# Expert tiles from a transposed copy in memory, and gate one-hots made eight tokens at a time with the gates multiplied in on ScalarE

## The chip, the cores and the metric

The kernel runs on one core of a Trainium2 chip. The metric is the device time of one execution in microseconds. A number comes from three executions and from one profiled execution.

## What is computed

One layer of an encoder for 1024 tokens of width 1024 in float32: attention heads, a recurrent group, and then a retrieval layer (PEER), which the change is about. For each token, 8 heads pick 16 each of 16384 experts; an expert is one row of `expert_u` and one row of `expert_v`.

```python
e_idx = i1[top] * 128 + i2[top]            # 8 heads x 16 experts of each token
gate = softmax(top_s)
u = take(expert_u, ic)                     # (tokens, 128, 1024)
act = gelu(einsum('cd,ced->ce', xc, u))
vv = take(expert_v, ic)
y = einsum('ce,ced->cd', gc * act, vv)
```

## The kernel before

The work up to the retrieval layer is not touched (lines up to 1323). The retrieval layer handles its tokens in two ways. Three blocks of 128 tokens (`NGB = 3`) are gathered: `gather_tasks` (1355) fetches for token block and expert slot the 128 rows of `peer_u` that its tokens chose by an indirect DMA from GpSimd (`fetch`, 1359), multiplies and sums them on VectorE (1392), and adds 128 rows of `peer_v`, scaled, to an accumulator (1400). That makes 384 steps with a u fetch and a v fetch each; `gathers` hands them out in portions.

The other five blocks (640 tokens, `TD`) go the dense way: every one of the 16384 experts is evaluated for every token, and the gates, zero for an expert that was not chosen, decide what counts. The experts come as 128 tiles of 128. A tile is handled so:

- `u_load` (1437) brings 128 rows of `peer_u` (128x1024) on SP's queue; two buffers.
- `u_transpose` (1442) turns half of it, four 128x128 pieces, on TensorE into a PSUM bank named `put` (tag `a`, one of three banks that `pact` uses too); ScalarE copies the bank to `uTh` as rounded float32r (1452), VectorE subtracts that from the bank and leaves the remainder in `uTl` (1458).
- `act_half` (1460) makes for half of the 640 tokens the products uTh x dTh, uTh x dTl and uTl x dTh over 8 pieces (lines 317 to 319, tile `pact`), and ScalarE puts Gelu of them into `gl` (1467). For the 65 tiles named `early` the result goes to memory (`actd`).

`tile_steps` (1471) lists the steps of one tile with the load of the tile after next and the transposes of the next tile in it.

`merge` lays several lists of steps over each other, each over a given share of the whole; the order of the steps, and with it the order of each engine's instructions, comes from these lists, which a scheduling layer then follows closely. Four stretches follow each other, with times as in the profile:

1. About 1180 to 1360: queries of the first three blocks.
2. About 1360 to 1950: queries of the others, the lists of chosen experts (`c_steps`), 45 early tiles and the first 74 gather steps.
3. About 1950 to 2380, the gate stage: `g_steps` (1690) makes the dense table of gates in memory, `Gd`, block by block; 20 early tiles and 60 gather steps run beside it.
4. From 2380, the dense stage: the remaining 63 tiles, `gate` (1790: GpSimd multiplies `gl` with the table, ScalarE and VectorE split it into `ah` and `al`), and the products with the v tiles (`one`, 1823, tile `py`, lines 1835 to 1837), which VectorE adds up every four tiles (1844). GpSimd makes the remainder `vl` of each v tile (1815). The gathers go on.

In `g_steps` an expert number is taken apart into row i and column j of a 128x128 grid, and for one token the gates are the product of two one-hot matrices with the 128 chosen experts as the contracted index: `o1` holds the gate where the row matches, `o2` a 1 where the column matches. `prep` makes the transposed tables `tT` (rows, columns, gates, and the negated gates and rows). `hot` (1710) makes the one-hots of eight tokens; `mm` (1733) makes eight 128x128 products (1741) into two PSUM banks `pgb`, from which ScalarE copies them into `st` (1744); `store` writes `st` to `Gd`. There are 80 such groups of eight, and two buffers of `o1` and `o2` each.

The work of `hot` is shared out: all eight `o2` at once on VectorE (1714); of the eight `o1` four on VectorE, two on GpSimd (1720), two on ScalarE, as an absolute value and then a Relu (1726, 1730). `MIX` says which:

```python
MIX = "DDDDPPAA"
eng = nc.vector if MIX[q] == "D" else nc.gpsimd
r_ = eng.tensor_scalar(o1[:, q], io128, tT[:, 0, t:t + 1], tT[:, 2, t:t + 1],
                       op0=ALU.is_equal, op1=ALU.mult)
if MIX[q] == "P":
    pace[0] = r_
```

`pace[0]` is the last GpSimd operation recorded; `fetch` orders each gather behind it on GpSimd, without a wait, so that gathers are spread over the stage. During the gate stage a gather has seven buffers for u and seven for v (four, and three more for this stage), later four each.

## Time and profile before

| | |
|---|---|
| three executions | 4042.25, 4057.2, 4059.28 us |
| median | 4057.2 us |
| profiled execution: its own time | 4056.53 us |
| profiled execution: its span | 4054.8 us |
| busy share of the span | TensorE 86%, VectorE 75%, GpSimd 57%, ScalarE 31% |
| mean granted clock of TensorE | 0.928 of full speed |
| moved between memory and the core | 862.81 MB, mean 213 GB/s |

PE is TensorE, DVE VectorE, ACT ScalarE, POOL GpSimd, and SP the queue of most loads and stores. A group of instructions is named by line, engine, operation and tiles, as out<-in, and given with its count, busy time, the mean of one and the idle time of its engine just before. Matrix products overlap in the engine's pipe, so their busy time is less than count times mean. The shares are means over stretches that differ; the stretches are read apart.

### The profile page before, as it was taken

The numbers are of one execution on the slowest core, as the hardware profiler recorded it, in microseconds if no ns is written. First come the engines' busy times: TensorE is split into PE (matmuls) and PEld (weight loads), VectorE is DVE, ScalarE is ACT, GpSimd is POOL, SyncE is SP. The second block draws the span as 40 slices with busy tenths as digits, with TensorE's granted clock in tenths as the row PEclk, the third lists the DMA queues.
The fourth block names the chain that finished last, engine by engine and source line by source line (L and its number), as shares of the span: only waits on it lengthen the run. The fifth ranks groups of instructions, "written<-read, shape, count | busy, mean of one in ns | idle before, by whom it ended". The sixth has DMA issues, their size and how long they took to land. (4 is left out here: it accounts for less than half of the span.)

```text
span 4054.8 us, 62013 instructions
## 1 busy us (share of the span) xinstructions
PE 3468.1 (86%) x22961; PEld 3038.1 (75%) x22961; DVE 3047.6 (75%) x6082; ACT 1261.6 (31%) x2528; POOL 2316.8 (57%) x1762
## 2 busy tenths in 40 slices
PE   5978899988787878988888878889888988889898
PEld 4757877776787877878877766777777877777787
DVE  6776556776567999799788877777677878877765
ACT  3244344444213222222555532221222222222221
POOL 2132112221434466366699978777777877878774
PEclk9978998888898989999999989999899999999999
DMA  6543444343445366466798998777788888777774
GB/s 191 178 144 103 141 116 98 97 111 104 136 164 184 104 219 238 141 218 214 239 296 278 301 309 277 264 259 269 255 273 285 281 272 275 272 265 271 256 258 154
DMA packets 493462, 862.81 MB, mean 213 GB/s; under 512 B 149348, under 2 KB 290404, under 8 KB 489064
## 3 DMA queue, kind: packets, MB, share of 16 engines
q1 hardware_dynamic: 372840, 447.20, 34.3%
q0 software_dynamic: 113280, 411.63, 29.7%
q8 instruction: 181, 2.97, 0.3%
q10 hardware_dynamic: 7040, 0.03, 0.1%
q14 instruction: 121, 0.99, 0.1%
HBM read 741.91 MB, written 116.80 MB: 212 GB/s over the span
## 5 line engine op out<-in xcount | busy, mean ns | idle before, releaser
L1392 DVE SCALAR_TENSOR_TENSOR gu<-gu,ghr 128x1024 f32<-128x1024 f32 x384 | 590.3, 1538 | 301.5 <-DMA gu<-in_peer_u_dram,ei 296.2
L317 PE MATMUL pact<-dTh,uTh 128*128 128x320 f32 x2048 | 663.6, 324 | 72.2 <-DVE uTl L1458 68.3
L1400 DVE SCALAR_TENSOR_TENSOR gacc<-gv,gact,gacc 128x1024 f32<-128x1024 f32 x381 | 614.0, 1611 | 117.1 <-DMA gv<-in_peer_v_dram,ei 116.1
L319 PE MATMUL pact<-dTh,uTl 128*128 128x320 f32 x2048 | 651.3, 318 | 19.2 <-DVE uTl L1458 19.2
L318 PE MATMUL pact<-dTl,uTh 128*128 128x320 f32 x2048 | 650.3, 318 | 0.0
L1835 PE MATMUL py<-vh,ah 128*128 128x512 f32 x1280 | 531.7, 419 | 137.5 <-DVE yac L1844 77.4
L1364 POOL DMA_INDIRECT gu<-in_peer_u_dram,ei x384 | 517.9, 1349 | 86.2 <-issue 44.2
L1836 PE MATMUL py<-vl,ah 128*128 128x512 f32 x1280 | 529.1, 413 | 38.2 <-POOL vl L1815 38.2
L1364 POOL DMA_INDIRECT gv<-in_peer_v_dram,ei x384 | 477.9, 1245 | 115.0 <-issue 101.5
L1837 PE MATMUL py<-vh,al 128*128 128x512 f32 x1280 | 523.7, 409 | 4.5 <-DVE al L1796 4.5
L317 PEld LDWEIGHTS pact<-dTh,uTh 128*128 128x128 f32 x2048 | 400.8, 196 | 89.4 <-DVE uTl L1458 78.5
L1815 POOL TENSOR_TENSOR vl<-vr,vh 128x512 fp32r<-128x512 f32 x256 | 367.2, 1435 | 146.1 <-issue 116.5
L1835 PEld LDWEIGHTS py<-vh,ah 128*128 128x128 f32 x1280 | 254.9, 199 | 218.0 <-ACT vh L1814 68.8
L319 PEld LDWEIGHTS pact<-dTh,uTl 128*128 128x128 f32 x2048 | 400.1, 195 | 21.4 <-DVE uTl L1458 21.3
L318 PEld LDWEIGHTS pact<-dTl,uTh 128*128 128x128 f32 x2048 | 400.6, 196 | 2.6
L1836 PEld LDWEIGHTS py<-vl,ah 128*128 128x128 f32 x1280 | 255.2, 199 | 99.6 <-POOL vl L1815 51.4
L1467 ACT ACTIVATE gl<-pact 128x320 f32<-128x320 f32 x256 | 111.2, 437 | 632.8 <-PE pact L319 601.1
L1837 PEld LDWEIGHTS py<-vh,al 128*128 128x128 f32 x1280 | 255.2, 199 | 62.0 <-DVE al L1796 6.8
L1795 ACT ACTIVATE ah<-gl 128x640 fp32r<-128x640 f32 x128 | 92.7, 737 | 653.6 <-POOL gl L1794 552.0
L1720 POOL TENSOR_SCALAR o<-io,tT 128x128 f32<-128x128 f32 x160 | 232.5, 1457 | 35.7 <-ACT tT L164 27.5
L1741 PE MATMUL pgb<-o,o 128*128 128x128 f32 x1280 | 184.0, 290 | 64.8 <-POOL o L1720 56.4
L1814 ACT ACTIVATE vh<-vr 128x512 fp32r<-128x512 f32 x256 | 157.0, 624 | 226.3 <-PE py L1837 181.8
(1445 smaller groups left out, 7527.1 us busy)
## 6 DMA issues: line engine op xcount, KB each, us to landing
u<-in_peer_u_dram SPq DMA_DIRECT2D x128, 512.0 KB, 5.8
vr<-in_peer_v_dram SPq DMA_DIRECT2D x256, 256.0 KB, 4.0
Gd<-st SPq DMA_DIRECT2D x160, 256.0 KB, 7.1
actd<-gl SPq DMA_DIRECT2D x65, 320.0 KB, 4.4
gl<-actd SPq DMA_DIRECT2D x65, 320.0 KB, 4.8
awt<-in_ada_w_dram SPq DMA_DIRECT2D x32, 512.0 KB, 6.4
wraw<-in_peer_w_query_dram SPq DMA_DIRECT2D x32, 512.0 KB, 4.0
wraw<-in_w_in_dram SPq DMA_DIRECT2D x26, 512.0 KB, 5.1
```

What stands on the lines that cost most here:

```text
L317: nc.tensor.matmul(ps, lh, rh, start=(i == 0), stop=False)
L318: nc.tensor.matmul(ps, lh, rl, start=False, stop=False)
L319: nc.tensor.matmul(ps, ll, rh, start=False, stop=(i == n - 1))
L1364: g_ = nc.gpsimd.indirect_dma_start(out=r_, out_offset=None, in_=src, in_offset=bass.IndirectOffsetOnAxis(ap=eid[tb][:, j:j + 1], axis=0))
L1392: nc.vector.scalar_tensor_tensor(u, u, 1.0, hr, op0=ALU.mult, op1=ALU.mult, accum_out=act[:, q:q + 1])
L1400: nc.vector.scalar_tensor_tensor(acc, v, pact[:, q:q + 1], acc, op0=ALU.mult, op1=ALU.add)
L1720: r_ = eng.tensor_scalar(o1[:, q], io128, tT[:, 0, t:t + 1], tT[:, 2, t:t + 1], op0=ALU.is_equal, op1=ALU.mult)
L1741: nc.tensor.matmul(pg[:, q * 128:(q + 1) * 128], o1[:, 4 * x_ + q], o2[:, 4 * x_ + q], start=True, stop=True)
L1815: pace[0] = nc.gpsimd.tensor_tensor(vl, vts[i], vh, ALU.subtract)
L1835: nc.tensor.matmul(ys[hf][b], ah[:, ts], vh, start=(n == tiles[0]), stop=False)
L1836: nc.tensor.matmul(ys[hf][b], ah[:, ts], vl, start=False, stop=False)
L1837: nc.tensor.matmul(ys[hf][b], al[:, ts], vh, start=False, stop=(n == tiles[-1]))
```

## The change

The host makes a copy of `peer_u` in which tile n stands already transposed, as a new input (`in_peer_ut_dram`); `u_load` reads it, with 4 KB in each of 128 partitions as before. `u_split` takes the place of `u_transpose`: one copy of 128x1024 on ScalarE and one subtraction of 128x1024 on VectorE, from the loaded tile, and nothing on TensorE or in PSUM. In `hot` both one-hots are made by one wide comparison each on VectorE, and ScalarE multiplies the gate into each of the eight `o1` in place. GpSimd has no part in it, and `pace` is not set there. The gathers still read `peer_u` itself.

```diff
-ULP = (-1, 1)
-NUR = 1
-MIX = "DDDDPPAA"
...
         U, V = I["peer_u"][0], I["peer_v"][0]
-        Ue = U.rearrange("(a b) d -> b a d", b=128)
+        Ut = I["peer_ut"]
         Ve = V.rearrange("(a b) d -> b a d", b=128)
         TW = "tile"
         pe = ES()
...
                 next(gt, None)
-        uts, ats, urp = {}, {}, []
+        uts, ats = {}, {}
         early = [n for n in range(NT) if (n + 1) * NEARLY // NT > n * NEARLY // NT]
         seq = early + [n for n in range(NT) if n not in early]
         after = dict(zip(seq, seq[1:]))
         actd = dram.tile([NEARLY, 128, TD], F32, name="actd")
         def u_load(n):
+            if n in uts:
+                return
             u = lpa.tile([128, D], F32, name="u", bufs=NU)
-            nc.sync.dma_start(u, Ue[n])
+            nc.sync.dma_start(u, Ut[n])
             uts[n] = [u]
-        def u_transpose(n, kh):
-            if kh == 0:
-                uts[n] += [lpa.tile([128, NK, 128], FR, name="uTh"), lpa.tile([128, NK, 128], FR, name="uTl")]
-            u, uh, ul = uts[n]
-            pt = pa[0].tile([128, 512], F32, name="put", tag="a")
-            for i in range(4):
-                k = kh * 4 + i
-                nc.tensor.transpose(pt[:, i * 128:(i + 1) * 128], u[:, k * 128:(k + 1) * 128], ident)
-            ks = slice(kh * 4, kh * 4 + 4)
-            p3 = pt.rearrange("p (k e) -> p k e", k=4)
-            nc.scalar.activation(uh[:, ks], p3, AF.Copy)
-            if n in early and early.index(n) <= ULP[0] and kh >= ULP[1]:
-                ur = urp[0].tile([128, 512], F32, name="ur", bufs=NUR)
-                acp(ur, pt)
-                nc.gpsimd.tensor_tensor(ul[:, ks], ur.rearrange("p (k e) -> p k e", k=4), uh[:, ks], ALU.subtract)
-            else:
-                nc.vector.tensor_tensor(ul[:, ks], p3, uh[:, ks], ALU.subtract)
+        def u_split(n):
+            u_load(n)
+            if len(uts[n]) > 1:
+                return
+            u = uts[n][0]
+            uh, ul = lpa.tile([128, NK, 128], FR, name="uTh"), lpa.tile([128, NK, 128], FR, name="uTl")
+            u3 = u.rearrange("p (k e) -> p k e", k=NK)
+            nc.scalar.activation(uh, u3, AF.Copy)
+            nc.vector.tensor_tensor(ul, u3, uh, ALU.subtract)
+            uts[n] += [uh, ul]
         def act_half(n, hf):
+            u_split(n)
             _, uh, ul = uts[n]
             if hf == 0:
                 ats[n] = lpa.tile([128, TD], F32, name="gl", bufs=NGL)
...
             L = [lambda: act_half(n, 0), lambda: act_half(n, 1)]
             if n in after:
                 m = after[n]
-                L = [lambda: u_transpose(m, 0), L[0], lambda: u_transpose(m, 1), L[1]]
+                L = [lambda: u_split(m), L[0], lambda: None, L[1]]
                 if m in after:
-                    L[0] = lambda: (u_load(after[m]), u_transpose(m, 0))
+                    L[0] = lambda: (u_load(after[m]), u_split(m))
             return L
         with ES() as qs:
             q1 = qs.enter_context(tc.tile_pool(name="q1", bufs=1, reuse_waits=TW))
             q2 = qs.enter_context(tc.tile_pool(name="q2", bufs=2, reuse_waits=TW))
-            urp.append(q2)
             pq = qs.enter_context(tc.tile_pool(name="pq", bufs=5, space=PSUM, reuse_waits=TW))
             def qbank(name):
...
             for L in hl[:NGB]:
                 for f in L:
                     f()
-            u_transpose(seq[0], 0)
-            u_transpose(seq[0], 1)
+            u_split(seq[0])
             merge((Q1, 0, 1), (sum(hl[NGB:], []), 0.1, HE))
             cg, cd = [c_steps(tb) for tb in range(NGB)], [c_steps(tb) for tb in range(NGB, NB)]
             tl_ = [tile_steps(n) for n in early]
...
                     nc.tensor.transpose(pt[:, 128:256], fj[:, 1], ident)
                     nc.tensor.transpose(pt[:, 256:384], wgt[tb], ident)
-                    s["t"] = tT = g1.tile([128, 5, 128], F32, name="tT")
-                    acp(tT[:, 0:3].rearrange("p a b -> p (a b)"), pt[:, 0:384])
-                    nc.scalar.activation(tT[:, 3], pt[:, 256:384], AF.Copy, scale=-1.0)
-                    nc.scalar.activation(tT[:, 4], pt[:, 0:128], AF.Copy, scale=-1.0)
+                    s["t"] = tT = g1.tile([128, 3, 128], F32, name="tT")
+                    acp(tT.rearrange("p a b -> p (a b)"), pt[:, 0:384])
                 def hot(t8):
                     tT = s["t"]
                     t0 = t8 * 8
                     s[t8] = o1, o2 = [g1.tile([128, 8, 128], F32, name=n_, bufs=NHOT) for n_ in ("o1", "o2")]
-                    nc.vector.tensor_tensor(o2, io128[:, None, :].to_broadcast([128, 8, 128]),
-                                            tT[:, 1, t0:t0 + 8, None].to_broadcast([128, 8, 128]), ALU.is_equal)
+
+                    for i, o_ in enumerate((o1, o2)):
+                        nc.vector.tensor_tensor(o_, io128[:, None, :].to_broadcast([128, 8, 128]),
+                                                tT[:, i, t0:t0 + 8, None].to_broadcast([128, 8, 128]), ALU.is_equal)
                     for q in range(8):
-                        t = t0 + q
-                        if MIX[q] != "A":
-                            eng = nc.vector if MIX[q] == "D" else nc.gpsimd
-                            r_ = eng.tensor_scalar(o1[:, q], io128, tT[:, 0, t:t + 1], tT[:, 2, t:t + 1],
-                                                   op0=ALU.is_equal, op1=ALU.mult)
-                            if MIX[q] == "P":
-                                pace[0] = r_
-                        else:
-
-                            nc.scalar.activation(o1[:, q], io128, AF.Abs, bias=tT[:, 4, t:t + 1])
-                    for q in range(8):
-                        t = t0 + q
-                        if MIX[q] == "A":
-                            nc.scalar.activation(o1[:, q], o1[:, q], AF.Relu, scale=tT[:, 3, t:t + 1],
-                                                 bias=tT[:, 2, t:t + 1])
+                        nc.scalar.activation(o1[:, q], o1[:, q], AF.Copy, scale=tT[:, 2, t0 + q:t0 + q + 1])
                 def mm(t8):
                     if t8 % (TC // 8) == 0:
...
         a = _np.ascontiguousarray(inputs[name])
         arrays[f"in_{name}_dram"] = a
         args[name] = nc.dram_tensor(f"in_{name}_dram", a.shape, mybir.dt.from_np(a.dtype), kind="ExternalInput").ap()
+
+    a = inputs["peer_u"]
+    a = _np.ascontiguousarray(_np.asarray(a)[0].reshape(128, 128, NK, 128).transpose(1, 3, 2, 0)).reshape(128, 128, D)
+    arrays["in_peer_ut_dram"] = a
+    args["peer_ut"] = nc.dram_tensor("in_peer_ut_dram", a.shape, mybir.dt.from_np(a.dtype), kind="ExternalInput").ap()
     o = nc.dram_tensor("out_0_dram", (1, T, D), F32, kind="ExternalOutput").ap()
     with tile.TileContext(nc) as tc:
         body(tc, nc, args, o)
```

Two places of the order, in the gate stage. On POOL, GpSimd's queue, `o` is a tile of one-hots, and `gu` and `gv` are gathered rows. Before:

```order
L1364 DMA gv_21560<-in_peer_v_dram,ei0_11946 128x1024
L1720 TENSOR_SCALAR o1_21618<-io128_11962,tT_21614 128x128 x2
L1364 DMA gu_21642<-in_peer_u_dram,ei0_11946 128x1024
L1364 DMA gv_21644<-in_peer_v_dram,ei0_11946 128x1024
L1720 TENSOR_SCALAR o1_21648<-io128_11962,tT_21614 128x128 x2
L1720 TENSOR_SCALAR o1_21703<-io128_11962,tT_21614 128x128 x2
L1364 DMA gu_21718<-in_peer_u_dram,ei0_11946 128x1024
```

Now:

```order
L1361 DMA gv_19920<-in_peer_v_dram,ei0_11946 128x1024
L1361 DMA gu_19973<-in_peer_u_dram,ei0_11946 128x1024
L1361 DMA gv_19975<-in_peer_v_dram,ei0_11946 128x1024
L1361 DMA gu_20033<-in_peer_u_dram,ei0_11946 128x1024
L1361 DMA gv_20035<-in_peer_v_dram,ei0_11946 128x1024
L1361 DMA gu_20106<-in_peer_u_dram,ei0_11946 128x1024
```

The one-hots are gone from between the gathers; 65 pairs stand there in one piece.

On ACT, ScalarE's queue, in the same stage; `st` is the copy of products out of the bank `pgb`, `gl` the Gelu of a tile, `uTh` the rounded u tile. Before:

```order
L1726 ACTIVATE o_19765<-io_11962,tT 128x128 x2
L1730 ACTIVATE o_19765<-o_19765,tT 128x128 x2
L1467 ACTIVATE gl<-pact 128x320
L1744 ACTIVATE st<-pgb 128x128x4 x2
L1452 ACTIVATE uTh<-put 128x512
L1726 ACTIVATE o_19809<-io_11962,tT 128x128 x2
L1730 ACTIVATE o_19809<-o_19809,tT 128x128 x2
L1744 ACTIVATE st<-pgb 128x128x4 x2
L1726 ACTIVATE o_19870<-io_11962,tT 128x128 x2
```

Now:

```order
L1708 ACTIVATE o_19455<-o_19455,tT 128x128 x8
L1721 ACTIVATE st<-pgb 128x128x4 x2
L1448 ACTIVATE uTh<-u 128x1024
L1708 ACTIVATE o_19487<-o_19487,tT 128x128 x8
L1708 ACTIVATE o_19540<-o_19540,tT 128x128 x8
L1721 ACTIVATE st<-pgb 128x128x4 x4
L1460 ACTIVATE gl<-pact 128x320
L1708 ACTIVATE o_19578<-o_19578,tT 128x128 x8
L1721 ACTIVATE st<-pgb 128x128x4 x2
```

Four operations for two tokens of a group have become eight for its eight tokens, at one place the eight of two groups stand ahead of four copies out of PSUM, and two copies of half a u tile have become one of 128x1024.

## Rows read from the trace of the kernel before

**Rows 1.** The page, part 1: busy us, share of the span, instructions.

```profile
PE 3468.1 (86%) x22961; PEld 3038.1 (75%) x22961; DVE 3047.6 (75%) x6082; ACT 1261.6 (31%) x2528; POOL 2316.8 (57%) x1762
```

**Rows 2.** Stretches: start, end, length, then as the first line names them.

```profile
core 0: us, PE busy (x) PEld busy (x) DVE busy (x) ACT busy (x) POOL busy (x), PEclk, DMA share, GB/s
1360.00:1650.00 290.00, 240.21 (x1561) 235.53 (x1560) 268.80 (x872) 74.99 (x143) 155.84 (x103) 0.90 0.55 189
1650.00:1950.00 300.00, 255.88 (x1679) 248.11 (x1678) 278.79 (x761) 74.13 (x138) 162.33 (x108) 0.95 0.59 201
1950.00:2380.00 430.00, 356.75 (x2478) 335.83 (x2477) 354.35 (x633) 243.98 (x582) 380.92 (x278) 0.95 0.88 285
2380.00:4055.00 1675.00, 1469.15 (x7304) 1252.05 (x7304) 1243.83 (x1362) 355.48 (x658) 1269.41 (x896) 0.95 0.77 264
```

**Rows 3.** Waits in 1950 to 2380: who waited for whom, us, times, longest us.

```profile
PE pgb L1741 <- POOL o L1720: 56.4, 63, 2.2
...
DVE o L1714 <- PE pgb L1741: 17.1, 16, 1.9
```

**Rows 4.** Groups by line, 1950 to 2380: busy us, mean ns, idle before and releasers.

```profile
L1720 POOL TENSOR_SCALAR o<-io,tT 128x128 f32<-128x128 f32 x160 | 232.5, 1457 | 35.7 <-ACT tT L164 27.5 <-issue 6.2
...
L1714 DVE TENSOR_TENSOR o<-io,tT 128x1024 f32<-128x1024 f32 x80 | 98.7, 1234 | 27.9 <-PE pgb L1741 17.1 <-ACT tT L164 10.8
L1720 DVE TENSOR_SCALAR o<-io,tT 128x128 f32<-128x128 f32 x320 | 96.7, 389 | 0.0
...
L1364 POOL DMA_INDIRECT gv<-in_peer_v_dram,ei x59 | 74.4, 1261 | 18.0 <-issue 14.6 <-DVE o L1720 0.9 <-PE pgb L1741 0.9
L1364 POOL DMA_INDIRECT gu<-in_peer_u_dram,ei x59 | 74.0, 1254 | 10.0 <-issue 7.1 <-DVE o L1720 1.3 <-ACT st L1744 0.7
L1392 DVE SCALAR_TENSOR_TENSOR gu<-gu,ghr 128x1024 f32<-128x1024 f32 x59 | 72.4, 1227 | 22.5 <-DMA gu<-in_peer_u_dram,ei 17.4 <-DMA ghr<-h2d 5.0
L1730 ACT ACTIVATE o<-o,tT 128x128 f32<-128x128 f32 x160 | 69.7, 486 | 0.0
...
L1726 ACT ACTIVATE o<-io,tT 128x128 f32<-128x128 f32 x160 | 55.0, 396 | 0.1
L1458 DVE TENSOR_TENSOR uTl<-put,uTh 128x512 fp32r<-128x512 f32 x42 | 28.6, 680 | 6.5 <-ACT uTh L1452 6.5
...
L1452 ACT ACTIVATE uTh<-put 128x512 fp32r<-128x512 f32 x42 | 25.0, 596 | 10.5 <-PE put L1449 10.3
```

**Rows 5.** Groups by line, 2380 to 4055.

```profile
L1835 PE MATMUL py<-vh,ah 128*128 128x512 f32 x1280 | 531.7, 419 | 137.5 <-DVE yac L1844 77.4 <-ACT vh L1814 59.6
L1836 PE MATMUL py<-vl,ah 128*128 128x512 f32 x1280 | 529.1, 413 | 38.2 <-POOL vl L1815 38.2
...
L1392 DVE SCALAR_TENSOR_TENSOR gu<-gu,ghr 128x1024 f32<-128x1024 f32 x248 | 409.8, 1653 | 273.3 <-DMA gu<-in_peer_u_dram,ei 273.1
```

**Rows 6.** The same view and stretch: transposes of u, copies, subtractions.

```profile
L1458 DVE TENSOR_TENSOR uTl<-put,uTh 128x512 fp32r<-128x512 f32 x122 | 78.1, 678 | 0.9 <-ACT uTh L1452 0.5
L1452 ACT ACTIVATE uTh<-put 128x512 fp32r<-128x512 f32 x122 | 65.2, 584 | 0.7 <-PE put L1449 0.7
L1449 PE MATMUL put<-ident,u 128*128 128x128 f32 x488 | 64.4, 274 | 6.0 <-DVE uTl L1458 3.5 <-ACT gl L1467 2.4
```

**Rows 7.** Groups by line, whole span: 128x1024 copy and subtraction in other stages.

```profile
L1544 ACT ACTIVATE wh<-wraw 128x1024 fp32r<-128x1024 f32 x32 | 33.7, 1059 | 39.0 <-PE psz L318 31.5 <-DMA h2d<-h 7.3 <-POOL oe L1635 0.3
...
L175 DVE TENSOR_TENSOR wl<-wraw,wh 128x1024 fp32r<-128x1024 f32 x24 | 31.3, 1316 | 38.2 <-ACT wh L174 38.2
```

**Rows 8.** Timeline of ScalarE about 2153: start us, us, engine, line; a pair.

```profile
2153.46 0.69 ACT L1726 ACTIVATE o<-io,tT 128x128 f32<-128x128 f32 x2
```

**Rows 9.** Stretches again: 50 us in the gate stage.

```profile
2000.00:2050.00 50.00, 42.89 (x305) 40.81 (x304) 44.02 (x77) 27.94 (x68) 46.33 (x34) 0.97 0.95 314
```

**Rows 10.** Groups by line on VectorE, 1360 to 1950.

```profile
L1458 DVE TENSOR_TENSOR uTl<-put,uTh 128x512 fp32r<-128x512 f32 x89 | 60.3, 678 | 22.8 <-ACT uTh L1452 22.8
```

## The prediction, made before the changed kernel was run

> **What bounds the kernel now.** I read the page's busy shares first. TensorE is busy for 86% of the span, VectorE for 75% and GpSimd for 57% [rows 1], so the mean names TensorE. The table of stretches corrects this [rows 2]. In 1360 to 1950, where the retrieval lists are made beside 45 of the u tiles, VectorE is busy for 269 of 290 us and 279 of 300: VectorE bounds it. In 1950 to 2380, where the gates are scattered into a dense table, GpSimd is busy for 381 of 430 us, ahead of TensorE (357) and VectorE (354). In 2380 to 4055, the dense products, TensorE is busy for 1469 of 1675 us (88%) and no other engine passes 1270.
>
> The waits say who holds whom. In the gate stage the one-hot products on TensorE waited 56.4 us for GpSimd's share of the one-hots, and VectorE waited 17.1 us for those products to free its buffers [rows 3]; GpSimd's 160 one-hots take 1457 ns each, 232.5 us in all [rows 4]. In the dense stage TensorE's gaps are 206 us (1675 less 1469); two rows hold 176 of them, most of it behind VectorE's additions of the products, ScalarE's and GpSimd's halves of the v tiles [rows 5]. VectorE works in order, and stood 273 us there until a gathered row tile landed [rows 5]. So its waits are for transfers, but they reach TensorE through the additions behind them.
>
> **The change, part by part.** The sum is made against the profiled execution, 4056.5 us with a span of 4054.8; the median of the three runs is 4057.2, so 0.7 us lie between them. About 0.5%, 20 us, is what a measurement can tell from no change.
>
> *Dense stage, 2380 to 4055.* 488 transposes leave TensorE: 64.4 us busy and 6.0 us idle right before them [rows 6], 70.4 us together. TensorE does nothing else in that time and is the busiest engine, so I first take all of it as path. ScalarE's 122 copies of 584 ns become 61 of about 1.06 us, the duration of a 128x1024 copy out of SBUF elsewhere [rows 6, 7]; ScalarE was busy for 355 of 1675 us, so this is worth nothing by itself. VectorE's 122 subtractions (78.1 us) become 61 of 128x1024 with both inputs in SBUF. The same shape took 1316 ns in another stage [rows 7]: 61 x 1.32 = 80.5 us, 2 us more. But what reads two SBUF tiles is stretched in this stage: the gather's multiply-and-sum took 1653 ns here and 1227 in the gate stage, while the old subtraction, with one input in PSUM, took 678 and 680 in both [rows 4 to 6]. If the new subtraction is stretched by the same 0.43 us, VectorE gets 61 x 0.43 = 26 us more, and 29 in all. Half of that, 15 us, I give back, since the additions that TensorE waits for stand behind it on VectorE: **55 us gained**, between 70 (nothing given back) and 12 (VectorE's 29 us, and as much again on GpSimd, whose operation would be held likewise).
>
> The Trainium skill has a rule that speaks against this part: "SBUF — State Buffer", section "Who interferes with whom", says that a VectorE instruction with two SBUF inputs contends with a GpSimd instruction that reads SBUF, and that one with a single SBUF input does not. The two durations of the multiply-and-sum beside the constant subtraction agree with it. By the rule alone every split that meets a GpSimd operation is blocked, or blocks it, which is the 12 us end.
>
> *Gate stage, 1950 to 2380.* GpSimd loses its 232.5 us and keeps its share of the gathers, 74.4 + 74.0 us [rows 4]: it bounds nothing there. On POOL's queue the gathers now stand without one-hots between them (the order shows 65 pairs in one piece), so they go out as their seven buffers come free. VectorE loses 320 operations (96.7 us) and gets 80 more of the 128x1024 comparison at 1234 ns (98.7 us) [rows 4]; its u splits stay level (21 x 1.32 = 27.7 us against 28.6). VectorE stays at 354 us and becomes the busiest. ScalarE loses 69.7 + 55.0 + 25.0 us [rows 4] and gets 640 multiplies of 128x128 with one operand from memory, and 21 copies of 1.06 us. The nearest row for the multiply is the absolute value with one such operand, 396 ns alone, and a pair took 0.69 us [rows 4, 8], so each further one adds 0.30: eight take 0.40 + 7 x 0.30 = 2.5 us, 80 times 200 us. ScalarE goes from 244 to 244 - 150 + 200 + 22 = 316 us. TensorE loses its transposes there, behind other bounds.
>
> What is late next? VectorE's waits are 430 - 354 = 76 us now. The 17.1 us for the one-hot products were behind GpSimd, and the gathers run further ahead, so I leave it 46 of the 76: 400 us, **30 us gained**. The ends: the transfers of this stage are 285 GB/s x 430 us = 122.6 MB, and stretches where the DMA engines were 95% busy moved 314 GB/s [rows 2, 9], which makes 390 us the shortest (40 gained); and nothing gained, if VectorE keeps all its waits.
>
> The Trainium skill speaks against this part as well: "ScalarE: Activation LUTs", section "Rules for kernel authors", says to multiply on VectorE and not on ScalarE. By the rows, eight fused comparisons with multiplication on VectorE would be 8 x 96.7 / 320 = 2.4 us, against 1.23 us of VectorE for the wide comparison; 80 times the difference, 95 us, would lie on the engine that is the busiest there, so I don't follow it.
>
> *The stretch 1360 to 1950.* TensorE's transposes go, but VectorE bounds, so they are worth nothing. VectorE's 89 subtractions (60.3 us) become 44.5 x 1.32 = 58.7 us. They also stood 22.8 us idle for ScalarE's copy of the transposed tile [rows 10]; that copy now starts from a tile which was loaded one tile earlier, so part of this goes. **10 us gained**, between 24 (all of it) and 18 lost (each stretched by 0.43 us: 44.5 x 0.43 = 19, less 1.6).
>
> The loads stay 512 KB per tile on SP's queue, issued at the same step; the tile is free again after the split rather than after the transposes, a tile's time before it is needed. Table loads of ScalarE stay at 50 in the order, so nothing is added there.
>
> Sum: 55 + 30 + 10 = 95. 4056.5 - 95 = 3961.5, and I say **3960 us**.
>
> **The rivals.** *Slower: ScalarE becomes the bound of the gate stage.* Every one-hot now passes VectorE, then eight multiplies on ScalarE, then TensorE, and ScalarE, which also empties the products, works in order: in several places of its order sixteen multiplies stand ahead of four evacuations. If a multiply in place costs what the row with two operands shows, 69.7 / 160 = 0.436 us, they take 279 us and ScalarE is busy for 395. If it also keeps the 186 us that it stands idle now (430 - 244), the stage takes 581 us, 151 more; with 65 gained elsewhere that is 4143 us. Against it: ScalarE's idle time was mostly spent waiting for what GpSimd held up. It decides once busy and idle pass 515 us together.
>
> *The gathers set the pace of the dense stage.* VectorE's 1244 us and 273 us of waits for gathers already fill 1517 of 1675 us, and GpSimd issues the gathers among its own work of 1269 us. If they can't come sooner, TensorE's 70 us turn into longer waits at the additions: the 55 us are lost and the time is 4015.
>
> *The shared path, in full.* The rule above gives 12 instead of 55 us: 4005. For it: the stretch of 0.43 us in the mean. Against it: it needs both engines' losses on the path.
>
> *The gate stage stays.* VectorE keeps 354 us and the DMA engines are 88% busy already [rows 2]; if both keep the stage at 430, the time is 3990.
>
> *More than the sum.* Transposed pieces no longer take one of the three PSUM banks that the activations use, and VectorE's in-order stops ease; if a quarter of TensorE's 206 us of gaps goes too, 50 us, the time is 3910.
>
> That the change doesn't do what it says is excluded by the order: the transposes and GpSimd's one-hots are gone from it.
>
> **How the numbers follow.** Forecast (3925 to 3990) 0.46; more than the sum 0.12; gathers set the pace 0.12; gate stage stays 0.12; shared path in full 0.07; two of these losses together (about 4045) 0.06; slower 0.05. Faster by over 0.5% (below 4037) are all but the last two: 0.88, with 0.01 for their edges; within 0.5% 0.07; slower 0.05. The range 3895 to 4035 leaves out the last two and the lower tail of the case of more gain, some 0.16.
>
> **What would show it.** Right: no transposes of u on TensorE, the dense stage near 1620 us with TensorE's busy time down by about 65; the gate stage near 400 us with GpSimd below 160 us busy, VectorE near 354, ScalarE near 316, and one multiply near 0.40 us. Wrong: a split on VectorE above 1.7 us in the dense stage with longer waits of TensorE for the additions; waits of the one-hot products for ScalarE beyond the 56 us that GpSimd cost; or an unchanged wait of VectorE for gathers with TensorE's share falling.

## The result and the profile after

The changed kernel takes 3945.24 us (median of 4 executions, 3932.93 to 3949.59); the kernel before, run beside it, 4057.92 us (4 executions, 4042.25 to 4059.28). The ratio is 0.9727, with a 95% interval of 0.9699 to 0.9754. The forecast was 3960 us in a range of 3895 to 4035.

The profiled execution took 3945.48 us with a span of 3943.7. The page's part 1 of the kernel after (busy us, share, instructions):

```profile
PE 3337.1 (85%) x21937; PEld 2924.9 (74%) x21937; DVE 3093.7 (78%) x5714; ACT 1313.8 (33%) x2710; POOL 2171.6 (55%) x1602
```

Against [rows 1] TensorE has lost 131 us and GpSimd 145, VectorE has gained 46 and ScalarE 52, and the span is 111 shorter. To place this, both traces are cut at the same events and not at round times: the first of GpSimd's `oe` products in the list-making stretch, the first and the last one-hot product (`pgb`), the first and the last product of a v tile (`py`). First the three stretches before, then after:

```profile
1353.00:1954.90 601.90, 507.99 (x3320) 495.43 (x3320) 557.52 (x1672) 153.79 (x295) 326.15 (x217) 0.93 0.56 192
1954.90:2367.30 412.40, 343.18 (x2387) 322.79 (x2385) 344.65 (x617) 237.95 (x567) 376.48 (x275) 0.95 0.89 288
2389.60:4043.90 1654.30, 1462.51 (x7278) 1246.14 (x7279) 1235.85 (x1350) 354.21 (x656) 1266.90 (x894) 0.95 0.78 264
```

```profile
1345.40:1923.10 577.70, 475.41 (x3030) 466.11 (x3029) 564.65 (x1623) 144.08 (x251) 345.29 (x223) 0.92 0.62 206
1923.10:2297.40 374.30, 309.76 (x2194) 300.46 (x2193) 334.42 (x360) 303.47 (x857) 194.85 (x110) 0.92 0.94 311
2317.40:3932.80 1615.40, 1415.94 (x6790) 1201.89 (x6791) 1283.02 (x1288) 350.70 (x594) 1279.47 (x894) 0.93 0.77 270
```

Columns as in [rows 2]: length, then busy us of TensorE, its weight loads, VectorE, ScalarE and GpSimd, the granted clock, DMA share and GB/s. The lists take 24 us less, the gate stage 38, the dense stage 39. The other 10 us are 8 in code before 1353 us that the change doesn't touch, and 2 in the gap between the last two stretches.

The gate stage after, groups by line (1923 to 2297), which answer to [rows 4]:

```profile
L1708 ACT ACTIVATE o<-o,tT 128x128 f32<-128x128 f32 x635 | 192.6, 393 | 16.7 <-DVE o L1705 16.3
L1705 DVE TENSOR_TENSOR o<-io,tT 128x1024 f32<-128x1024 f32 x158 | 184.6, 1216 | 33.1 <-ACT tT L161 22.3 <-PE pgb L1718 10.8
...
L1361 POOL DMA_INDIRECT gv<-in_peer_v_dram,ei x55 | 105.4, 1916 | 42.8 <-DVE gacc L1397 27.9 <-DVE o L1705 8.5 <-issue 5.2
...
L1361 POOL DMA_INDIRECT gu<-in_peer_u_dram,ei x55 | 91.4, 1661 | 111.6 <-DVE gu L1389 103.4 <-DVE gacc L1397 4.3 <-issue 2.7
...
L1449 DVE TENSOR_TENSOR uTl<-u,uTh 128x1024 fp32r<-128x1024 f32 x18 | 21.8, 1213 | 0.0
L1448 ACT ACTIVATE uTh<-u 128x1024 fp32r<-128x1024 f32 x19 | 20.1, 1057 | 31.8 <-DMA u<-in_peer_ut_dram 30.5 <-PE pact L315 1.2
```

One multiply takes 393 ns. GpSimd no longer bounds: it stands 103 us until VectorE frees a buffer of gathered rows. VectorE is the busiest, 334 of 374 us. The last row is new: ScalarE's copy of the loaded u tile stands 30.5 us for a DMA. The waits of the same stretch (us, times, longest) tell who pays:

```profile
PEld pgb L1718 <- ACT o L1708: 43.7, 19, 11.6
ACT uTh L1448 <- DMA u<-in_peer_ut_dram: 30.5, 7, 11.2
...
PE pgb L1718 <- ACT o L1708: 25.1, 11, 11.3
DVE o L1705 <- ACT tT L161: 22.3, 4, 11.5
```

In [rows 3] the one-hot products waited 56.4 us for GpSimd. Now they wait 25.1 us for ScalarE's multiplies, in pieces of up to 11.3 us, the length of the copy's wait for the tile. ScalarE's timeline at one such piece, then SP's queue in the time before (start, us, engine, line):

```profile
2020.33 0.60 ACT L1721 ACTIVATE st<-pgb 128x512 f32<-128x512 f32 x1 [0.30 <-PE pgb L1718]
2032.12 1.06 ACT L1448 ACTIVATE uTh<-u 128x1024 fp32r<-128x1024 f32 x1 [11.19 <-DMA u<-in_peer_ut_dram]
2033.08 4.77 ACT L1708 ACTIVATE o<-o,tT 128x128 f32<-128x128 f32 x16
2037.75 2.02 ACT L1721 ACTIVATE st<-pgb 128x512 f32<-128x512 f32 x4
```

```profile
2011.60 5.63 SPq L1730 DMA_DIRECT2D Gd<-st  x6
2017.33 1.29 SPq L1462 DMA_DIRECT2D actd<-gl  x1
2018.96 3.81 SPq L1730 DMA_DIRECT2D Gd<-st  x2
2022.88 2.46 SPq L1438 DMA_DIRECT2D u<-in_peer_ut_dram  x1
```

ScalarE stands from 2020.9 to 2032.1, and sixteen multiplies and four evacuations stand behind the copy. The load it waits for was issued only at 2022.88, behind eight stores of gate tables and one of a Gelu tile. Those stores wait for ScalarE (SP's own waits, same stretch):

```profile
SPq L1730 <- ACT st L1721: 41.8, 7, 15.8
SPq L1730 <- ACT gl L1460: 39.4, 4, 15.9
SPq L1462 <- ACT gl L1460: 27.3, 5, 7.7
SPq L1462 <- ACT o L1708: 24.3, 10, 8.1
```

So this reads as a loop: a store waits for ScalarE, the load waits behind the store, ScalarE waits for the load. In the trace of before, a load went out 28 us before its own tile was first transposed, in the median of 19 tiles, and landed after 5.8 us; no wait for it is listed there. Now it goes out 9 us after the copy of the tile ahead (2142.1 behind 2133.1) and 9.5 us before its own; the median is 9.6. A load of before, for the tile first transposed at 2167.4, then one of after and the copy that uses its tile:

```profile
2138.61 0.35 SPq L1439 DMA_DIRECT2D u<-in_peer_u_dram  x1
...
2142.14 0.63 SPq L1438 DMA_DIRECT2D u<-in_peer_ut_dram  x1
...
2151.61 1.06 ACT L1448 ACTIVATE uTh<-u 128x1024 fp32r<-128x1024 f32 x1 [0.51 <-DMA u<-in_peer_ut_dram]
```

The dense stage after (2317 to 3933), which answers to [rows 5, 6]:

```profile
L1813 PE MATMUL py<-vl,ah 128*128 128x512 f32 x1279 | 533.1, 417 | 56.7 <-POOL vl L1792 56.7
L1812 PE MATMUL py<-vh,ah 128*128 128x512 f32 x1280 | 528.8, 417 | 138.6 <-ACT vh L1791 91.7 <-DVE yac L1821 43.6 <-ACT gl L1460 2.7
...
L1389 DVE SCALAR_TENSOR_TENSOR gu<-gu,ghr 128x1024 f32<-128x1024 f32 x248 | 448.1, 1807 | 200.9 <-DMA gu<-in_peer_u_dram,ei 198.9 <-issue 1.4 <-DMA ghr<-h2d 0.4
...
L1449 DVE TENSOR_TENSOR uTl<-u,uTh 128x1024 fp32r<-128x1024 f32 x60 | 109.6, 1827 | 0.0
```

The transposes are gone, yet TensorE's busy time fell by 47 us only (1462.5 to 1415.9), and its gaps grew from 192 to 199 us. Part of the 64.4 us of the transposes lay over other matmuls, which busy time counts once; that this is all of the difference is not shown, as the granted clock also fell, from 0.95 to 0.93. The new subtraction takes 1827 ns here against 1213 in the gate stage, and the multiply-and-sum went from 1653 to 1807. One of them in time, VectorE's timeline and then GpSimd's:

```profile
2475.62 1.21 DVE L1389 SCALAR_TENSOR_TENSOR gu<-gu,ghr 128x1024 f32<-128x1024 f32 x1
...
2477.97 2.31 DVE L1449 TENSOR_TENSOR uTl<-u,uTh 128x1024 fp32r<-128x1024 f32 x1
```

```profile
2475.66 2.00 POOL L1361 DMA_INDIRECT gv<-in_peer_v_dram,ei  x1 [0.30 <-issue]
2477.67 1.52 POOL L1792 TENSOR_TENSOR vl<-vr,vh 128x512 fp32r<-128x512 f32 x1
```

Beside the issue of a gather a VectorE operation on two SBUF tiles takes 1.21 us; beside GpSimd's subtraction, which reads SBUF and was begun 0.3 us before, the split takes 2.31 us. Its excess, 1.1 us, is about what GpSimd's operation still had to run (1.2 us). The 60 splits of the stage fall into two groups: 28 took 1.21 to 1.25 us and 32 took 2.28 to 2.60 us. Each of the 32 began while one of GpSimd's products or subtractions (`gl`, `vl`) was already running; the 28 met an issue of a gather, an operation that began behind them, or nothing.

How this reaches TensorE is told by its waits. Those for VectorE's additions (`yac`) fell from 77.4 [rows 5] to 43.6 us. Those for ScalarE's `vh` rose from 59.6 to 91.7, for GpSimd's `vl` from 38.2 to 56.7. One piece in time, over all engines:

```profile
2651.35 2.51 POOL L1771 TENSOR_TENSOR gl<-gl,gt__24504 128x640 f32<-128x640 f32 x1
2652.39 2.55 DVE L1449 TENSOR_TENSOR uTl<-u,uTh 128x1024 fp32r<-128x1024 f32 x1
2653.89 1.36 ACT L1772 ACTIVATE ah<-gl 128x640 fp32r<-128x640 f32 x2 [7.96 <-POOL gl L1771]
2655.16 1.13 ACT L1791 ACTIVATE vh<-vr 128x512 fp32r<-128x512 f32 x2
2655.83 0.80 PE L1812 MATMUL py<-vh,ah 128*128 128x512 f32 x1 [4.06 <-ACT vh L1791]
```

GpSimd's product `gl` takes 2.51 us here and 1.57 where no VectorE operation ran as it began. The split waits behind it, ScalarE stands for it in front of `ah`, the copies of v tiles stand behind `ah`, and TensorE stands for those. In 41 of the 92 us that TensorE waited for `vh`, ScalarE stood so; before the change in 24 of 60.

### The profile page after: what moved, and what is told of

It reads as the page before. It is cut to its first block, busy times and chain, and to the rows that moved or that the text cites. A ratio compares the mean times of both kernels' runs of the same rounds, so it can differ in the third digit from the quotient of the medians.

```text
span 3943.7 us, 59658 instructions
## 1 busy us (share of the span) xinstructions
PE 3337.1 (85%) x21937; PEld 2924.9 (74%) x21937; DVE 3093.7 (78%) x5714; ACT 1313.8 (33%) x2710; POOL 2171.6 (55%) x1602
## 5 line engine op out<-in xcount | busy, mean ns | idle before, releaser
L1389 DVE SCALAR_TENSOR_TENSOR gu<-gu,ghr 128x1024 f32<-128x1024 f32 x384 | 631.3, 1645 | 211.9 <-DMA gu<-in_peer_u_dram,ei 203.1
L1361 POOL DMA_INDIRECT gu<-in_peer_u_dram,ei x384 | 575.6, 1499 | 184.2 <-DVE gu L1389 116.5
L314 PE MATMUL pact<-dTh,uTh 128*128 128x320 f32 x2048 | 650.3, 318 | 23.9 <-ACT uTh L1448 11.3
L1397 DVE SCALAR_TENSOR_TENSOR gacc<-gv,gact,gacc 128x1024 f32<-128x1024 f32 x381 | 586.1, 1538 | 95.2 <-DMA gv<-in_peer_v_dram,ei 87.8
L1812 PE MATMUL py<-vh,ah 128*128 128x512 f32 x1280 | 528.8, 417 | 138.6 <-ACT vh L1791 91.7
L1361 POOL DMA_INDIRECT gv<-in_peer_v_dram,ei x384 | 504.2, 1313 | 147.6 <-issue 90.9
L1813 PE MATMUL py<-vl,ah 128*128 128x512 f32 x1280 | 533.5, 417 | 56.7 <-POOL vl L1792 56.7
L1448 ACT ACTIVATE uTh<-u 128x1024 fp32r<-128x1024 f32 x128 | 135.2, 1057 | 262.2 <-PE pact L315 203.1
L1705 DVE TENSOR_TENSOR o<-io,tT 128x1024 f32<-128x1024 f32 x160 | 186.9, 1216 | 33.1 <-ACT tT L161 22.3
L1718 PE MATMUL pgb<-o,o 128*128 128x128 f32 x1280 | 175.8, 292 | 39.1 <-ACT o L1708 25.1
```

The source lines that it names most:

```text
L314: nc.tensor.matmul(ps, lh, rh, start=(i == 0), stop=False)
L1361: g_ = nc.gpsimd.indirect_dma_start(out=r_, out_offset=None, in_=src, in_offset=bass.IndirectOffsetOnAxis(ap=eid[tb][:, j:j + 1], axis=0))
L1389: nc.vector.scalar_tensor_tensor(u, u, 1.0, hr, op0=ALU.mult, op1=ALU.mult, accum_out=act[:, q:q + 1])
L1397: nc.vector.scalar_tensor_tensor(acc, v, pact[:, q:q + 1], acc, op0=ALU.mult, op1=ALU.add)
L1705: nc.vector.tensor_tensor(o_, io128[:, None, :].to_broadcast([128, 8, 128]), tT[:, i, t0:t0 + 8, None].to_broadcast([128, 8, 128]), ALU.is ...
L1718: nc.tensor.matmul(pg[:, q * 128:(q + 1) * 128], o1[:, 4 * x_ + q], o2[:, 4 * x_ + q], start=True, stop=True)
```

## The experiments

Theory after the first reading: the two parts are each worth more than the whole shows. In the gate stage the late u tile on the in-order ScalarE eats what the gate part gives; in the dense stage the two-input subtraction eats what the missing transposes give. Rivals: the DMA engines bound the gate stage; the depth of the gather buffers does; the transposes were hidden anyway. Lengths of the three stretches by the same events, and the times:

| kernel | lists | gate | dense | span | median us | ratio to before (95%) |
|---|---|---|---|---|---|---|
| before | 601.9 | 412.4 | 1654.3 | 4054.8 | 4057.92 | |
| after | 577.7 | 374.3 | 1615.4 | 3943.7 | 3945.24 | 0.9727 (0.9699 to 0.9754) |
| e1_u_only | 573.8 | 429.0 | 1613.4 | 3998.2 | 3993.13 | 0.9847 (0.9815 to 0.9879) |
| e2_gate_only | 608.1 | 330.9 | 1651.9 | 3973.6 | 3976.01 | 0.9805 (0.9765 to 0.9845) |
| e3_load_ahead | 580.2 | 341.2 | 1607.9 | 3907.8 | 3913.24 | 0.9670 (0.9651 to 0.9689) |
| e4_idle_transposes | 577.9 | 371.8 | 1641.5 | 3976.5 | 3975.70 | 0.9806 (0.9773 to 0.9839) |
| e5_psum_subtract | 579.7 | 375.7 | 1576.0 | 3913.1 | 3912.16 | 0.9662 (0.9621 to 0.9702) |
| e6_four_buffers | 576.9 | 371.4 | 1624.8 | 3954.5 | 3943.32 | 0.9737 (0.9714 to 0.9761) |
| e7_vector_gates | 576.0 | 407.4 | 1602.5 | 3967.2 | 3973.44 | 0.9822 (0.9802 to 0.9843) |
| e8_half_stores | 577.5 | 340.2 | 1613.9 | 3902.9 | 3907.04 | 0.9658 (0.9638 to 0.9678) |
| e9_both_mended | 577.5 | 341.5 | 1578.2 | 3877.5 | 3877.28 | 0.9579 (0.9550 to 0.9609) |
| e10_pool_loads | 578.1 | 354.1 | 1614.7 | 3927.4 | 3930.75 | 0.9704 (0.9670 to 0.9738) |

### The two parts alone

The u part without the gate part: the changed kernel with `prep`, `hot` and `MIX` of before. The gate part without the u part: the kernel before with the new `prep` and `hot`.

> The u part of the change alone; the gates are made as before, with GpSimd's share. If the two parts add up, this holds the 24 us of the list stretch and the 39 us of the dense stage: 4058 - 63 = 3995 us, with the gate stage (first to last one-hot product) between 405 and 412 us, since GpSimd still bounds it. Rival: GpSimd's relief in the gate stage let the gathers run ahead and made the dense stage shorter; then the dense stage stays above 1640 us here and the time is about 4020.

> The gate part alone; the u tiles are transposed on TensorE as before. If the parts add up: 4058 - 40 = 4018 us, the gate stage near 375 us and the dense stage near 1655. Rival: the gate stage is short only because TensorE's transposes and their PSUM traffic left it too; then it stays above 395 us and the time is above 4035.

The u part alone gives 28 us in the lists and 41 in the dense stage, and costs 17 in the gate stage, where GpSimd is still the bound (397 us busy) and the products wait 76.6 us for its one-hots in place of 56.4; why those became slower was not tried. In the trace, the 20 of them that ran beside a two-input split took 2.20 us in the mean, and before the change the 37 beside a split took 1.27; this fits, but is no test. The gate part alone gives 81 us in the gate stage, far more than expected, and moves the other two by 6 and 2. The gate stage of e2:

```profile
1960.10:2291.00 330.90, 313.91 (x2380) 304.87 (x2381) 324.23 (x364) 302.22 (x880) 151.52 (x95) 0.99 1.00 334
```

VectorE is busy 324 of 331 us, and the DMA engines moved 334 GB/s at a share of 1.00. Together the parts would give 17 - 81 = -65 us there; the whole kernel shows -38. The 27 us between are the parts' disagreement, all of it in this stage.

### Late u tiles: earlier loads, another queue

e3 loads each u tile of the gate stage one tile earlier, with a third buffer in the stage's own pool:

```diff
-u = lpa.tile([128, D], F32, name="u", bufs=NU)
+third = ug and EARLY[1] + 2 < seq.index(n) < NEARLY - 2 and seq.index(n) % 3 == 0
+u = ug[0].tile([128, D], F32, name="u3", bufs=1) if third else lpa.tile([128, D], F32, name="u", bufs=NU)
...
-L[0] = lambda: (u_load(after[m]), u_split(m))
+far = EARLY[1] <= seq.index(n) and seq.index(n) + 3 < NEARLY
+L[0] = lambda: (u_load(after[m]), far and u_load(after[after[m]]), u_split(m))
...
+ug.append(g1)
```

> The changed kernel, with the u tiles of the gate stage loaded one tile earlier, into a third buffer. ScalarE waited 30.5 us there for a u tile to land, in front of its multiplies. If that wait is on the path, it falls below 5 us and the gate stage (374 us) falls by 15 to 25 us. Rival: the transfers themselves bound the stage (DMA engines 94% busy, 311 GB/s); then the wait moves to another transfer and the stage stays within 6 us of 374.

e10 keeps buffers and places in the order and changes the queue alone:

```diff
-nc.sync.dma_start(u, Ut[n])
+gates = EARLY[1] <= seq.index(n) < NEARLY
+(nc.gpsimd if gates else nc.sync).dma_start(u, Ut[n])
```

> The change as it is, but the 20 u tiles of the gate stage are issued on GpSimd's queue in place of SP's; no more buffers and no earlier place in the order. If the tiles come late because their loads stand on SP's queue behind stores that wait for ScalarE, the loads now go out as soon as a buffer and GpSimd are free, the copy waits clearly less than 30 us for them, and the gate stage falls from 374 towards 341 us, the time to 3915 to 3930. Rival: they come late because the second buffer comes free late, or because the DMA engines are full; then the queue doesn't matter, the wait stays near 30 us and the stage near 374. A third way: GpSimd's queue is itself held by gathers that wait for their buffers, the loads come later still, and the stage goes above 385.

The gate stage of e3 and the copy's wait for a load in it (us, times, longest), then two waits of ScalarE in the gate stage of e10:

```profile
1928.30:2269.50 341.20, 300.12 (x2194) 289.38 (x2194) 333.26 (x359) 302.75 (x854) 197.07 (x109) 0.98 1.00 341
...
ACT uTh L1449 <- DMA u<-in_peer_ut_dram: 1.6, 1, 1.6
```

```profile
ACT st L1722 <- DMA Gd<-st: 13.4, 3, 10.3
...
ACT uTh L1449 <- PE pact L315: 3.9, 5, 1.2
```

In e3 the stage is 33 us shorter at the same work, and the copy's wait for a load is 1.6 us. In e10 no wait for a load is left before the copy, only 3.9 us for products that free its buffer, and the stage is 20 us shorter, with nothing changed but the queue. The loads go out 15.5 us before their use in the median (9.6 in the change, 22.8 in e3). So the place behind the stores on SP's queue made the tiles late: shown, for 20 of the 33 us. The other 13 us that e3 has over e10 are not taken apart; e10 has a wait of its own, 13.4 us of the evacuations for stores to finish.

e8 writes and reads half of the gate table's transfers:

```diff
-stores.extend(lambda i=i: store(st, i, 128 // TC * b + t8 * 8 // TC) for i in range(NST))
+stores.extend(lambda i=i: store(st, i, 128 // TC * b + t8 * 8 // TC) for i in range(0, NST, 2))
...
-nc.sync.dma_start(gts[q], Gd[q])
+nc.sync.dma_start(gts[q], Gd[q - TC // NST * (q * NST // TC % 2)])
```

> The changed kernel, with every second store of the gate table left out and the loads of the table directed to the stored half, so that half of the gates are wrong: 20 of 117 MB leave the gate stage. If the transfers bound it, it falls with the bytes, from 374 towards the 340 us of VectorE: 340 to 355. If VectorE with its order bounds it, within 8 us of 374.

```profile
1921.80:2262.00 340.20, 297.96 (x2197) 287.49 (x2195) 334.39 (x360) 302.99 (x858) 195.86 (x110) 0.98 0.86 285
```

The stage is as short as e3's, with 285 GB/s against 341. By the words of the expectation this is the mark of a bound by transfers; e3 speaks against that. The copy's wait for a load is 6.0 us here. Fewer stores ahead of the loads give what earlier loads give, and e3 gets it with all bytes moved, so the bytes are not the bound of the changed kernel; VectorE, with 333 to 334 us in both, is what is left.

### Gather buffers, and the multiply on VectorE

e6 takes the three more gather buffers of the gate stage away (`NXG = 0`).

> The changed kernel, with four buffers each for the gathered rows in the gate stage as in the other stages, not seven. If gathers that run far ahead crowd out the u tiles and the stores, ScalarE's wait for u tiles falls from 30 to below 15 us and the stage gets shorter by 5 to 15 us. If depth hides the gathers' own latency, VectorE waits for gathers again (28 us before the change, none after it) and the stage grows by 10 to 30 us.

Neither came: 371 us in the gate stage, 28.8 us of the copy's waits for u tiles, no wait of VectorE for gathered rows, and a ratio whose interval overlaps that of the change. The depth is worth nothing here, and GpSimd's waits for buffers (148 us against 131) cost nothing. The dense stage is 9 us longer in the profiled execution, where the others with the same code in it (after, e1, e3, e7, e8, e10) lie between 1602.5 and 1615.4 us; the median is not longer, and the cause is open.

e7 makes `o1` with a fused compare and multiply on VectorE, token by token, and nothing on ScalarE:

```diff
-nc.scalar.activation(o1[:, q], o1[:, q], AF.Copy, scale=tT[:, 2, t0 + q:t0 + q + 1])
+nc.vector.tensor_scalar(o1[:, q], io128, tT[:, 0, t0 + q:t0 + q + 1], tT[:, 2, t0 + q:t0 + q + 1],
+                        op0=ALU.is_equal, op1=ALU.mult)
```

> The changed kernel, with the gates multiplied in on VectorE: eight fused comparisons of 128x128 for each group in place of the second wide comparison and ScalarE's multiplies. By the rows of before, 80 x (2.4 - 1.2) = 96 us more of VectorE and 193 us less of ScalarE. If VectorE is the busiest engine of the stage, its 334 us become 430 and the stage grows from 374 to 435 to 460 us: total near 4015. Rival: ScalarE and the transfers bound the stage; then it grows by less than 30 us.

```profile
1927.80:2335.20 407.40, 326.87 (x2206) 314.55 (x2207) 406.88 (x918) 129.99 (x223) 154.33 (x109) 0.91 0.89 287
```

VectorE is busy for all of 407 us, 33 more than the stage of the change; the span is 23.5 us longer than that of the change, the median 28. The loss is smaller than expected for two reasons. VectorE's busy time grew by 72 us and not 96; back to back the fused form is 351 ns in the mean, below the 389 of [rows 4]. And the 40 us that VectorE stood idle in the stage of the change are gone. Against e3, whose tiles come in time, the stage is 66 us longer. The Trainium skill ("ScalarE: Activation LUTs", "Rules for kernel authors") says to multiply on VectorE; here, where VectorE is the busiest engine, the runs go against it.

### The dense stage

e4 puts the transposes of the 63 dense tiles back on TensorE, into banks that nobody reads:

```diff
+if n not in early:
+    for kh in range(2):
+        pt = pa[0].tile([128, 512], F32, name="put", tag="a")
+        for i in range(4):
+            k = kh * 4 + i
+            nc.tensor.transpose(pt[:, i * 128:(i + 1) * 128], u[:, k * 128:(k + 1) * 128], ident)
```

> The changed kernel, with eight transposes of each u tile of the dense stage put back on TensorE, into banks that nobody reads. If TensorE's own time is what the dense stage gained, it grows by the 47 us by which TensorE's busy time fell, to about 1660 us, and the total to about 3990. If the gathers or the shared path set the pace, the transposes fit into TensorE's gaps: below 1630 us, total below 3960.

```profile
L1456 PE MATMUL put<-ident,u 128*128 128x128 f32 x488 | 64.9, 275 | 1.5 <-ACT gl L1466 1.4
```

The dense stage grows by 26 us, between the two expectations, and TensorE's busy time by 48, of the 64.9 that the group sums. In the changed kernel, part of the transposes would fit into gaps.

e5 gives the subtraction one SBUF input again: for the dense tiles ScalarE copies u into the free PSUM banks and VectorE subtracts from there.

```diff
-nc.vector.tensor_tensor(ul, u3, uh, ALU.subtract)
+if n in early:
+    nc.vector.tensor_tensor(ul, u3, uh, ALU.subtract)
+else:
+    for kh in range(2):
+        ks = slice(kh * 4, kh * 4 + 4)
+        pt = pa[0].tile([128, 512], F32, name="put", tag="a")
+        p3 = pt.rearrange("p (k e) -> p k e", k=4)
+        nc.scalar.activation(p3, u3[:, ks], AF.Copy)
+        nc.vector.tensor_tensor(ul[:, ks], p3, uh[:, ks], ALU.subtract)
```

> The changed kernel, but for the tiles of the dense stage ScalarE also copies u into two PSUM banks, and VectorE subtracts from there in two halves, so that it has one SBUF input as before the change. ScalarE gets 60 x 1.2 us more. If the stretch of the subtraction (1827 ns against 1216 at best) costs time, VectorE's part falls from 110 to about 82 us, GpSimd's products with VectorE get shorter too, and the dense stage falls by 10 to 25 us, to 1590 to 1605. If VectorE's stretch lies beside the path: within 8 us of 1616, or longer through ScalarE's extra work in front of the v tiles.

Its dense stage: the stretch, then groups by line.

```profile
2326.20:3902.20 1576.00, 1406.07 (x6790) 1194.78 (x6791) 1264.90 (x1350) 416.77 (x716) 1256.63 (x894) 0.95 0.80 277
```

```profile
L1820 PE MATMUL py<-vh,ah 128*128 128x512 f32 x1280 | 524.8, 414 | 110.1 <-ACT vh L1799 64.7 <-DVE yac L1829 42.4 <-ACT gl L1468 2.7
...
L1457 DVE TENSOR_TENSOR uTl<-put,uTh 128x512 fp32r<-128x512 f32 x122 | 78.5, 678 | 0.0
L1456 ACT ACTIVATE put<-u 128x512 f32<-128x512 f32 x122 | 72.3, 594 | 6.5 <-DVE uTl L1457 4.6
```

ScalarE is busy 66 us more (the copies alone make 72), and the stage is 39 us shorter, more than expected: the subtraction is at 678 ns per half again, as in [rows 6], VectorE is busy 18 us less, GpSimd 23 less, and TensorE waits 27 us less for `vh`; its wait for the additions stays (42.4 us against 43.6). ScalarE stood for `gl` in 20 us of the waits for `vh`, 21 less than in the change. Some 10 of the 39 us are TensorE's busy time, at a granted clock of 0.95 against 0.93. By the medians the whole is 33 us, by the ratios 26.

### Both mended

e9 is e3 and e5 in one kernel.

> The load-ahead of the gate stage (33 us faster there) and the copy into PSUM of the dense stage (39 us faster there) in one kernel. If the late u tiles and the two-input subtraction are two separate losses in two separate stages, they add: gate stage near 341, dense stage near 1572, time near 3945 - 32 - 33 to 39 = 3875 us (ratio to the kernel before near 0.956). If either gain rests on the other stage being late (gathers ahead or behind at the seam), less than 40 us comes together, 3900 or above.

```profile
1927.60:2269.10 341.50, 297.68 (x2180) 286.57 (x2178) 334.30 (x361) 303.48 (x859) 195.72 (x110) 0.99 1.01 342
```

The two add: gate stage 341.5, dense stage 1578.2, 3877.28 us, ratio 0.9579 (0.9550 to 0.9609). By the spans it is 66 us faster than the change, 33 + 37 in the two stages less what the rest scatters, and it is the fastest of all that ran.

## Why the prediction was right, and which terms were not

By the spans 111 us were gained where 95 were said. That this is so near is in part luck: the dense stage was put 16 us too high, the gate stage 8 and the lists 14 too low, and 10 us lie outside the three stretches.

**What bounds each stage: right.** The gate part alone takes 81 us out of the gate stage, GpSimd falls from 376 to 152 us busy there (e2), and VectorE takes over. In the lists VectorE keeps its work (558 and 565 us busy), and the stretch is shorter by what it had waited.

**Dense stage, 55 said, 39 measured.** The stretch held: the split takes 1.83 us in the mean (1.75 said), VectorE's subtractions take 31 us more (29 said). The step that failed is "Half of that, 15 us, I give back", in its size and in its path. e5 shows 39 us given back, some 10 of them at a higher granted clock; without the stretch the stage gains 78 (1654.3 to 1576.0), 56 of TensorE's busy time and 22 of its gaps, where 70 were said. The path was to be the additions that stand behind the split on VectorE. But the waits for these fell to 43.6 us and e5 leaves them so; what e5 takes away are waits for `vh`, behind GpSimd's products and ScalarE's `ah`. So the sign "a split above 1.7 us with longer waits for the additions" came by half. TensorE's term and VectorE's are not separate: with the stretched split the transposes are worth 26 us (e4), without it about all of theirs. The Trainium skill's rule ("SBUF — State Buffer", "Who interferes with whom") agrees: the pair of rows at 2477 shows the split held for about as long as GpSimd's SBUF-reading operation still ran, and one PSUM input ends it.

**Gate stage, 30 said, 38 measured: two misses that nearly cancel.** The steps "I leave it 46 of the 76" and the transfers' floor of 390 us were both too dear: in e2 VectorE idles 7 us, and the DMA engines moved 334 to 342 GB/s in e2, e3 and e9, where I had taken 314 from a stretch at a share of 0.95. That is 81 us instead of 30. The other way went "the loads stay 512 KB per tile on SP's queue, issued at the same step": that was costed at nothing. The step is the same, but the load goes out some 9 us late in it, behind stores that wait for ScalarE, and so 9.6 us before its use and not "a tile's time", some 19 us; the engine that stands for a late tile is now ScalarE, with sixteen multiplies behind the copy. e3 prices that at 33 us, e10 at 20 for the queue alone. That the two parts each run without the loop (e2 waits for no tile at all, e1's copies for none either) fits it; why the stores come later than in e2 was not taken further apart. VectorE near 354 us was said, and 334 measured.

**Lists, 10 said, 24 measured.** The subtraction in 1345 to 1923:

```profile
L1449 DVE TENSOR_TENSOR uTl<-u,uTh 128x1024 fp32r<-128x1024 f32 x46 | 61.1, 1329 | 2.8 <-ACT uTh L1448 2.8
```

VectorE's wait for the copy fell from 22.8 us [rows 10] to 2.8. I had said that part of it goes; nearly all did, the upper end. At 1329 ns the split is hardly stretched there, so little was given back.

**Duration of the multiply: right** (0.40 said, 0.393 measured), and ScalarE with it (316 said, 303.5). GpSimd was put below 160 us and shows 195: its issues of gathers went from 1254 and 1261 ns to 1661 and 1916. Why was not tried; it waits for buffers 131 us beside that, so it holds nobody.

**The rivals.** ScalarE did not become the bound by its work, as the row of 486 ns feared, but the shape of that rival (multiplies in order, products behind them) is what cost 33 us, by a DMA and not by a duration; the products' wait for ScalarE, 25.1 us, stayed below the 56 that were named as a sign. The shared path in full put 58 us lost in the dense stage, and by e5 39 were; its way, by losses of GpSimd too, is nearer to what the waits show than the forecast's. "The gathers set the pace" did not come: VectorE's wait for gathered u rows fell from 273 to 199 us, and TensorE's wait for the additions fell too. "More than the sum" was not met: TensorE's gaps in the dense stage grew, from 192 to 199 us. e9 is below its 3910 us, but by two edits that are not in the change.

## What to carry to other kernels

When a step is moved from one engine to another, ask who now stands still if its input is late, and what is queued behind that engine; follow the load back on its own queue to see whether it stands behind stores that wait for the same engine. Where GpSimd computes beside VectorE, give VectorE operands of which one is in PSUM, even at the price of a copy on an idle engine. A sum of parts over different stages is safe only where no part changes what another part waits for: run the parts alone.

## What was not expected of the hardware

With all of the DMA engines' time in use (share 1.00) the stage moved 334 to 342 GB/s, 6 to 9% more than the 314 at a share of 0.95 had let expect. In the changed kernel's gate stage TensorE's granted clock was 0.92, in e2, e3, e8, e9 and e10 it was 0.97 to 0.99, and in e1 and e7 0.89 and 0.91; for each of these it is one profiled execution, and what made the difference was not tried.

The mean of the stretched split, 1.83 us, is a duration that none of them has: 28 of 60 took 1.21 to 1.25 us and 32 took 2.28 to 2.60, and which it was went by whether GpSimd's operation had begun first.
